# Two passes over the output weights: begun one set earlier, the second at three and four products a piece

## The chip, the cores and the metric

The kernel runs on one core of a Trainium2 chip. The metric is the device time of one execution in microseconds (us). A run of the kernel is told by the median of several executions; the profile is one more execution, recorded by the hardware profiler.

The engines are named as the profile names them: PE multiplies matrices (PEld is the loading of its stationary operand, which runs beside it), DVE is VectorE, ACT is ScalarE, POOL is GpSimd, SP is SyncE, which here only issues DMAs.

## The reference, cut to what matters

One decoder layer over x of 1024 tokens by 2048 features, in float32:

```python
h = einsum('bsd,dc->bsc', x, w_in) + b_in
q, k, v, g_attn, u_pool, g_pool = split(h)
a = banded_sink_attention(q, k, v, ...) * silu(g_attn)      # 16 heads, blocks of 128 queries
b = multiscale_pool(u_pool, w_pool, pool_scale) * silu(g_pool)
mix = einsum('bsc,cd->bsd', concatenate([a, b]), w_out)      # the output weights: w_out
ple = sigmoid(einsum('bsd,de->bse', x, w_gate_ple)) * einsum('bsp,pd->bsd', p_i, w_ple)
return layer_norm(2**0.25 * x + mix + ple, ln_gain, ln_bias)
```

The layer norm subtracts the mean over the 2048 features. So the mean over the output features may be taken out of each row of `w_out` beforehand. The kernel does that for the 1024 rows of the attention half (`a`): it writes a centred copy `wc` of these weights, which it reads instead of `w_out` in its last two stages.

## The kernel before, in words

**Jobs and products.** The large matrix products (with `w_in`, `w_gate_ple`, `w_out`) are cut into jobs. A job makes two blocks of 128 output features for 2 x 512 tokens, from half of the input features, in seven products instead of eight (Strassen's scheme in Winograd's form). So its operands are sums and differences of blocks: on the weights' side `s1` and the differences written over `raw` (`make_unit`), on the side of x the tiles `b11, b21, t1, t2, t3, b22, t4` (`set_from`). A float32 operand is split into a high and a low part (`wh` and `wl`, `b11h` and `b11l`, ...): ACT writes the high part, DVE the low one. A product is then 12 matmuls of 128x128 by 128x512: four slices of the contraction, three matmuls each, on lines 179 (high by high), 180 (wh by the low part of x) and 181 (wl by the high part of x). A unit is the pair `wh`, `wl` of one product; four units are made ahead of PE.

**Groups and sets.** Jobs run in groups of one to three. Jobs that run together alternate product by product. Group 0 holds three jobs (21 products), groups 1 and 2 two jobs each (14 products each); after those most groups are one job. The first two groups work on the first half of the contraction (the first set). During group 1 the second set is fetched, and during groups 1 and 2 its seven operands are made on ACT and DVE (the steps `s0` to `s4` of `set_from`). From group 3 on, attention (`heads`, 16 times, nine products apart) runs between the products of the large matrices. Its k and v are built twice (`k_build`, `v_build`), for the first and for the second group of heads.

**Banks.** A product accumulates in a bank of PSUM, `qa` or `qb`, each there twice. After it, ACT copies it into a tile `part` (L346) or DVE adds it (L122, `part<-part,qb`). A further product can begin in a bank only when that has been read. Transposes go to one bank `tr` that is there once: `trans` of attention uses it (ACT copies the high part, L544, then DVE makes the low part, `s<-tr,s`), and `v_build` (L457) too.

**Order.** A clock counts products: `tick` runs after each one what is due then. `after(n, fn)` puts `fn` at n products from now; `later` does the same and keeps its instructions behind the newest marked ones of each engine. So the place of each side task is a number in the code. The framework then orders each engine's instructions and adds the waits. Every engine works its list strictly in order, SP too: a DMA whose buffer isn't free holds up every DMA behind it.

**The two passes of `centre_weights`.** The weights come in 32 pieces of 128x512 (16 output blocks b, two halves h). There is one buffer for a piece, `cw`. First pass: for each piece a load (`fetch`, on SP) and two products later a row sum on DVE (`add_up`, L723), into `wsum`. Then the mean (`take_mean`). Second pass: the same load, two products later the subtraction on DVE in place (`centre`, L733, shown as L122 `cw<-cw,wmean`) and the store into `wc` on SP. Since `cw` is there once, the load of a piece waits for the row sum of the one before, and in the second pass for the end of the store before. In the kernel before, the passes are queued at clock 49, behind group 2 (`self.centre_weights(8, 3)`): first load due at 57, a piece every 2 products to 121; second pass from 123, at 2 products a piece where b is a multiple of 3 and at 3 otherwise, last subtraction due at 207.

Of the kernel before, what the change touches and what calls it, by code (L numbers as in the profile page):

```python
# [63 lines left out]
class Layer:  # L64
# [98 lines left out]
    def later(self, n, fn):  # L163

        def run():
            with ExitStack() as ctx:
                for ins in self.latest.values():
                    ctx.enter_context(self.tc.issue_after(ins))
                fn()
        self.after(n, run)  # L170
# [536 lines left out]

    def centre_weights(self, at, by):  # L710

        nc = self.nc
        cells = [(b, h) for b in range(NB) for h in range(2)]
        sums = self.fix.tile([P, 8, NB], F32, name="wsum")
        mean = self.fix.tile([P, 8], F32, name="wmean")
        now = []

        def fetch(b, h):
            now.append(self.load(self.tile(self.cw, [P, H], "cw"), self.wout[b, 0][:, h * H : h * H + H]))

        def add_up(b, h):
            k = now.pop().rearrange("p (k m) -> p k m", k=4)
            nc.vector.reduce_sum(sums[:, 4 * h : 4 * h + 4, b : b + 1], k, axis=mybir.AxisListType.X)  # L723

        def take_mean():
            nc.vector.reduce_sum(mean.rearrange("p (k b) -> p k b", b=1), sums, axis=mybir.AxisListType.X)
            nc.vector.tensor_scalar(out=mean, in0=mean, scalar1=1.0 / D, scalar2=None, op0=ALU.mult)

        def centre(b, h):
            w = now.pop()  # L730
            k = w.rearrange("p (k m) -> p k m", k=4)
            m = mean[:, 4 * h : 4 * h + 4].rearrange("p (k m) -> p k m", m=1).broadcast_to([P, 4, P])
            self.tt(k, k, m, ALU.subtract)  # L733
            self.load(self.wc[b, 0][:, h * H : h * H + H], w)

        for step in (add_up, centre):
            for c in cells:
                self.after(at, lambda c=c: fetch(*c))
                self.later(at + 2, lambda c=c, step=step: step(*c))
                at += by if step is centre and c[0] % 3 else 2  # L740
            if step is add_up:
                self.later(at + 1, take_mean)
                at += 2
# [96 lines left out]
    def run(self):  # L840
# [147 lines left out]
        nc.gpsimd.tensor_scalar(out=self.b8, in0=self.c(C_BIN, 8), scalar1=0.125, scalar2=1.0, op0=ALU.mult, op1=ALU.mult)  # L988
        begin, *steps = self.set_from(xs[1], T)
        begin()  # L990
        self.run_group(1)


# [8 lines left out]
        def build_kv(b, build, group):  # L1002
            src = [self.slot()[:, :T] for h in range(2)]
            for h in range(2):
                self.aside(src[h], kvd[b][:, h * T : h * T + T])
            self.later(2, lambda: build(group, src))
# [5 lines left out]
            self.after(t - 2 + 9 * i, lambda i=i: self.heads(i % 2, i // 2))  # L1012
        self.after(t + 63 + 8, lambda: build_kv(KB, self.k_build, 1))
        self.after(t + 63 + 22, lambda: build_kv(VB, self.v_build, 1))
        self.centre_weights(8, 3)
        begin, *steps = self.set_kept(xs[0], kept)
        for i in range(1, n2):
            if i == n2 - 1:
# [212 lines left out]
```

## Time and profile before

| what | value |
|---|---|
| time, median of 3 executions (lowest, highest) | 1488.71 us (1487.96, 1489.05) |
| the profiled execution's own time | 1488.72 us |
| its span | 1486.9 us |
| busy: PE, DVE, ACT, POOL | 1447.6, 1118.7, 779.5, 278.1 us |
| mean granted clock of PE | 0.992 |
| row sums on DVE (L723) | 32, from 174.3 to 376.4 us, median 680 ns |
| subtractions on DVE (`cw<-cw,wmean`) | 32, from 391.8 to 667.2 us, median 686 ns |

A busy PE isn't a PE at its best: a matmul of 128x512 is shown as about 390 ns long but they follow each other every 227 ns, so the busy times overlap. What the profile shows as a loss on PE is idle time, and a granted clock under 1.00. The profiled execution's time is 1.8 us over its span.

### The profile page before, as it was taken

Reading aid. Unit: us, or ns where it says so; the run is one execution under the profiler, and the core shown is the slowest. Engines: PE = TensorE matmul, PEld = TensorE weight load, DVE = VectorE, ACT = ScalarE, POOL = GpSimd, SP = SyncE. Lnnn points to the kernel's source line nnn. Section 1 sums busy time; section 2 is a strip of 40 time slices with the busy share of each in tenths; the row PEclk is TensorE's granted clock in tenths of the full one; section 3 lists DMA queues with packets and bytes.
Section 4 is the critical chain, followed back from the end, with each engine's and each line's share of the span. In section 5 each row is a group of like instructions: output and inputs, shape, how many; then the busy total and the mean of one; then the engine's idle time right before and its main releaser. Section 6 shows DMA issues by size and latency. Waiting matters only on the chain. (4 is left out here: it accounts for less than half of the span.)

```text
span 1486.9 us, 20458 instructions
## 1 busy us (share of the span) xinstructions
PE 1447.6 (97%) x6972; PEld 1223.5 (82%) x6972; DVE 1118.7 (75%) x2019; ACT 779.5 (52%) x1548; POOL 278.1 (19%) x388
## 2 busy tenths in 40 slices
PE   8999999999999999999999999999999999999996
PEld 6788888888887888888887778888877788899986
DVE  7788578888797878888667956565669666987786
ACT  5454666655666555666534443333256333554485
POOL 0000123332332333231111110000011111111231
PEclk9999999999999999999999999999999999999998
DMA  7563875445545455457856676666696768585464
GB/s 264 198 226 94 254 207 183 149 158 179 174 170 178 163 183 186 175 190 250 200 139 201 156 233 182 180 178 184 183 294 174 190 175 235 136 256 121 151 233 163
DMA packets 101913, 280.38 MB, mean 189 GB/s; under 512 B 11504, under 2 KB 17008, under 8 KB 101808
## 3 DMA queue, kind: packets, MB, share of 16 engines
q1 hardware_dynamic: 79024, 204.87, 40.3%
q0 software_dynamic: 19456, 66.86, 19.4%
q10 hardware_dynamic: 3328, 7.34, 1.5%
q8 instruction: 55, 0.90, 0.2%
q14 instruction: 50, 0.41, 0.1%
HBM read 193.04 MB, written 85.98 MB: 188 GB/s over the span
## 5 line engine op out<-in xcount | busy, mean ns | idle before, releaser
L222 ACT CAST wh<-raw 128x512 fp32r<-128x512 f32 x428 | 264.2, 619 | 448.6 <-PE qa L180 143.6
L122 DVE TENSOR_TENSOR wl<-raw,wh 128x512 fp32r<-128x512 f32 x428 | 299.5, 704 | 132.3 <-ACT wh L222 127.6
L346 ACT COPY part<-qa 128x512 f32<-128x512 f32 (+1 forms) x180 | 103.7, 576 | 56.5 <-PE qa L181 52.1
L551 POOL TENSOR_SCALAR_AFFINE_SELECT s<-s 128x512 fp32r<-128x512 f32 x128 | 100.6, 797 | 141.0 <-ACT s L544 98.3
L122 DVE TENSOR_TENSOR part<-part,qb 128x512 f32<-128x512 f32 (+1 forms) x120 | 80.9, 674 | 49.7 <-PE qb L181 47.0
L179 PE MATMUL qa<-b11h,wh 128*128 128x512 f32 (+2 forms) x292 | 111.2, 381 | 2.0 <-ACT b11h L248 1.5
L180 PE MATMUL qa<-b11l,wh 128*128 128x512 f32 (+2 forms) x292 | 110.2, 377 | 0.2 <-DVE b11l L122 0.2
L181 PE MATMUL qa<-b11h,wl 128*128 128x512 f32 (+2 forms) x292 | 109.8, 376 | 0.0
L179 PE MATMUL qb<-b21h,wh 128*128 128x512 f32 (+2 forms) x292 | 109.6, 375 | 0.0
L181 PE MATMUL qb<-b21h,wl 128*128 128x512 f32 (+2 forms) x292 | 109.2, 374 | 0.0
L180 PE MATMUL qb<-b21l,wh 128*128 128x512 f32 (+2 forms) x292 | 109.1, 374 | 0.0
L181 PE MATMUL qa<-t2h,wl 128*128 128x512 f32 (+1 forms) x260 | 100.0, 386 | 7.6 <-DVE wl L122 7.6
L179 PE MATMUL qa<-t2h,wh 128*128 128x512 f32 (+1 forms) x260 | 100.7, 388 | 5.3 <-ACT part L346 2.7
L179 PE MATMUL qb<-t1h,wh 128*128 128x512 f32 (+1 forms) x260 | 101.6, 391 | 3.5 <-DVE part L122 1.9
L181 PE MATMUL qb<-t1h,wl 128*128 128x512 f32 (+1 forms) x260 | 100.4, 386 | 1.5 <-DVE wl L122 1.5
L179 PE MATMUL qa<-t4h,wh 128*128 128x512 f32 (+1 forms) x260 | 100.3, 386 | 0.3 <-DVE part L122 0.3
L179 PE MATMUL qa<-t3h,wh 128*128 128x512 f32 (+1 forms) x260 | 100.5, 387 | 0.0
L180 PE MATMUL qb<-t1l,wh 128*128 128x512 f32 (+1 forms) x260 | 100.4, 386 | 0.0
L179 PE MATMUL qb<-b22h,wh 128*128 128x512 f32 (+1 forms) x260 | 100.3, 386 | 0.0
L180 PE MATMUL qb<-b22l,wh 128*128 128x512 f32 (+1 forms) x260 | 99.7, 384 | 0.0
L180 PE MATMUL qa<-t3l,wh 128*128 128x512 f32 (+1 forms) x260 | 99.7, 384 | 0.0
L181 PE MATMUL qb<-b22h,wl 128*128 128x512 f32 (+1 forms) x260 | 99.7, 383 | 0.0
(287 smaller groups left out, 3553.9 us busy)
## 6 DMA issues: line engine op xcount, KB each, us to landing
raw<-in_win SPq DMA_DIRECT2D x65, 512.0 KB, 4.0
h<-part SPq DMA_DIRECT2D x34, 512.0 KB, 2.9
part<-h POOLq DMA_DIRECT2D x34, 512.0 KB, 6.2
cw<-in_wout SPq DMA_DIRECT2D x64, 256.0 KB, 2.9
raw<-in_wgate SPq DMA_DIRECT2D x32, 512.0 KB, 4.4
raw<-wc SPq DMA_DIRECT2D x32, 512.0 KB, 4.1
s<-in_x SPq DMA_DIRECT2D x44, 256.0 KB, 5.7
wc<-cw SPq DMA_DIRECT2D x32, 256.0 KB, 2.3
```

Source lines behind the costliest of these rows:

```text
L122: return (eng or self.nc.vector).tensor_tensor(out=out, in0=a, in1=b, op=op)
L179: mm(ps, wh, xh, start=start, stop=False, skip_group_check=True)
L180: mm(ps, wh, xl, start=False, stop=False, skip_group_check=True)
L181: return mm(ps, wl, xh, start=False, stop=stop, skip_group_check=True)
L222: self.unit_latest = [nc.scalar.copy(out=hi, in_=src).ins, L.lo(lo, src, hi).ins]
L346: self.mark("ACT", self.nc.scalar.copy(out=dst, in_=ps))
L551: nc.gpsimd.affine_select(out=o4, in_=a4, pattern=[[0, 4], [sign, P]], compare_op=ALU.is_ge, fill=0.0, base=0 if side else -1, channel_mul ...
```

## The change

Three things change. `centre_weights` is queued behind group 0 (clock 21) instead of behind group 2 (clock 49), and its first load is due 2 products later instead of 8: at 23 instead of 57. The first pass keeps 2 products a piece and ends at 87. The second pass begins at 89, at 3, 4, 4, 4 products a piece in turn; its last subtraction stays due at 207. The instructions are the same in number and kind.

```diff
-    def centre_weights(self, at, by):
+    def centre_weights(self, at):
...
         for step in (add_up, centre):
-            for c in cells:
+            for i, c in enumerate(cells):
                 self.after(at, lambda c=c: fetch(*c))
                 self.later(at + 2, lambda c=c, step=step: step(*c))
-                at += by if step is centre and c[0] % 3 else 2
+                at += 2 if step is add_up else 3 + (i % 4 > 0)
             if step is add_up:
                 self.later(at + 1, take_mean)
                 at += 2
...
         begin()
+        self.centre_weights(2)
         self.run_group(1)
...
-        self.centre_weights(8, 3)
         begin, *steps = self.set_kept(xs[0], kept)
```

The lists of PE and POOL are the same before and after, instruction by instruction. Those of DVE, ACT and SP differ. In the rows below a name's number tells buffers apart and has no other meaning.

**DVE in group 2**, where the second set's operands are made: the low part of t2 (`t2l`), the units (`wl`), the sums and differences of the weights (`s1`, `raw`), and the reading of the bank of the job's second product (`part<-part,qb`). Before:

```order
L122 TENSOR_TENSOR wl_289_1095<-raw_269_998,wh_288_1094 128x512
L122 TENSOR_TENSOR s1_291_1112<-raw_264_962 128x512
L122 TENSOR_TENSOR t2l_305_1185<-two_236_813,t2h_304_1184 128x1024
L122 TENSOR_TENSOR raw_264_962<-raw_221_720,raw_264_962 128x512
L122 TENSOR_TENSOR wl_293_1118<-s1_291_1112,wh_292_1117 128x512
L122 TENSOR_TENSOR raw_221_720<-s1_291_1112,raw_221_720 128x512
L122 TENSOR_TENSOR s1_297_1143<-raw_270_1000 128x512
L122 TENSOR_TENSOR raw_221_720<-raw_221_720 128x512
L122 TENSOR_TENSOR raw_270_1000<-raw_269_998,raw_270_1000 128x512
L122 TENSOR_TENSOR wl_299_1149<-s1_297_1143,wh_298_1148 128x512
L122 TENSOR_TENSOR raw_269_998<-s1_297_1143,raw_269_998 128x512
L122 TENSOR_TENSOR part_280_1076<-part_280_1076,qb_300_1152 128x512
```

The same stretch of DVE's list now:

```order
L122 TENSOR_TENSOR wl_296_1117<-raw_273_1011,wh_295_1116 128x512
L122 TENSOR_TENSOR s1_298_1134<-raw_267_972 128x512
L122 TENSOR_TENSOR t2l_314_1213<-two_236_815,t2h_313_1212 128x1024
L122 TENSOR_TENSOR raw_267_972<-raw_221_720,raw_267_972 128x512
L122 TENSOR_TENSOR wl_300_1140<-s1_298_1134,wh_299_1139 128x512
L122 TENSOR_TENSOR raw_221_720<-s1_298_1134,raw_221_720 128x512
L723 TENSOR_REDUCE wsum_790<-cw_286_1096 128x4
L122 TENSOR_TENSOR raw_221_720<-raw_221_720 128x512
L122 TENSOR_TENSOR s1_305_1168<-raw_274_1013 128x512
L122 TENSOR_TENSOR part_287_1098<-part_287_1098,qb_308_1177 128x512
```

A row sum (L723) stands in it, and the reading of the bank has moved ahead of the difference over `raw` of the second job, of the unit behind it and of one more difference.

**SP in groups 1 and 2**: the loads of the weights (`raw<-in_win`), the stores of the first set's partial products (`h<-part`) and the loads of pieces (`cw<-in_wout`). Before:

```order
L136 DMA h_6_99<-part_154_323 128x1024
L136 DMA raw_264_962<-in_win 128x1024
L136 DMA raw_269_998<-in_win 128x1024
L136 DMA raw_270_1000<-in_win 128x1024
L136 DMA raw_273_1019<-in_win 128x1024
L136 DMA h_7_100<-part_228_790 128x1024
L136 DMA h_9_102<-part_230_792 128x1024
L136 DMA h_8_101<-part_229_791 128x1024
L136 DMA h_10_103<-part_231_793 128x1024
L136 DMA raw_318_1270<-in_win 128x1024
```

And now:

```order
L136 DMA h_6_99<-part_154_323 128x1024
L136 DMA cw_251_889<-in_wout 128x512
L136 DMA cw_260_932<-in_wout 128x512
L136 DMA raw_267_972<-in_win 128x1024
L136 DMA cw_268_975<-in_wout 128x512
L136 DMA raw_273_1011<-in_win 128x1024
L136 DMA raw_274_1013<-in_win 128x1024
L136 DMA cw_275_1016<-in_wout 128x512
L136 DMA raw_278_1035<-in_win 128x1024
L136 DMA h_7_100<-part_228_792 128x1024
L136 DMA h_9_102<-part_230_794 128x1024
L136 DMA cw_281_1055<-in_wout 128x512
```

Each load of a piece now stands between these loads and stores; it waits for the row sum of the piece before it, and holds up what stands behind it.

**DVE where k and v are built for the second group of heads**. The rows around the subtraction of a piece (`cw<-cw,wmean`) some products ahead of it, before:

```order
L514 TENSOR_SCALAR st_897_4373<-st_897_4373 128x4
L122 TENSOR_TENSOR st_897_4373<-cst_75,st_897_4373 128x4
L122 TENSOR_TENSOR part_923_4508<-part_923_4508,qa_926_4513 128x512
L122 TENSOR_TENSOR cw_938_4599<-cw_938_4599,wmean_1411 128x512
L122 TENSOR_TENSOR wl_955_4684<-raw_849_4120,wh_954_4683 128x512
L122 TENSOR_TENSOR s1_962_4718<-raw_891_4349 128x512
```

And now:

```order
L514 TENSOR_SCALAR st_905_4405<-st_905_4405 128x4
L122 TENSOR_TENSOR st_905_4405<-cst_75,st_905_4405 128x4
L122 TENSOR_TENSOR part_930_4538<-part_930_4538,qa_933_4543 128x512
L122 TENSOR_TENSOR wl_962_4710<-raw_857_4152,wh_961_4709 128x512
L122 TENSOR_TENSOR s1_968_4742<-raw_899_4379 128x512
L122 TENSOR_TENSOR st_905_4405<-st_905_4405 128x2
```

The subtraction between the reading of the bank and the unit is gone from here. Some rows further, at the low part of the transposed probabilities (`s<-tr,s`), whose end frees `tr` for `v_build`, DVE's list before:

```order
L122 TENSOR_TENSOR raw_849_4120<-raw_849_4120 128x512
L122 TENSOR_TENSOR wl_964_4724<-raw_849_4120,wh_963_4723 128x512
L525 RECIPROCAL st_897_4373<-st_897_4373 128x2
L122 TENSOR_TENSOR cw_959_4705<-cw_959_4705,wmean_1411 128x512
L122 TENSOR_TENSOR s_967_4748<-tr_965_4742,s_966_4747 128x512
L122 TENSOR_TENSOR wl_975_4778<-s1_962_4718,wh_974_4777 128x512
L122 TENSOR_TENSOR v0_971_4772<-tr_970_4767,v0_971_4772 128x4x64
```

And now:

```order
L122 TENSOR_TENSOR raw_857_4152<-raw_857_4152 128x512
L122 TENSOR_TENSOR wl_970_4748<-raw_857_4152,wh_969_4747 128x512
L122 TENSOR_TENSOR cw_960_4705<-cw_960_4705,wmean_791 128x512
L122 TENSOR_TENSOR st_905_4405<-st_905_4405 128x2
L122 TENSOR_TENSOR wl_981_4804<-s1_968_4742,wh_980_4803 128x512
L122 TENSOR_TENSOR s_973_4774<-tr_971_4768,s_972_4773 128x512
L525 RECIPROCAL st_905_4405<-st_905_4405 128x2
L122 TENSOR_TENSOR v0_977_4798<-tr_976_4793,v0_977_4798 128x4x64
```

Here a subtraction still stands ahead of `s<-tr,s`, and so does now the unit that stood behind it.

## The prediction

> **What bounds the kernel now.** I read the page first, then busy times by stage, then what PE waited for in the stages that the change reaches, then the tile `cw` and the neighbourhood of the one long wait.
>
> ```profile
> span 1486.9 us, 20458 instructions
> PE 1447.6 (97%) x6972; PEld 1223.5 (82%) x6972; DVE 1118.7 (75%) x2019; ACT 779.5 (52%) x1548; POOL 278.1 (19%) x388
> ```
>
> PE is the bound: its list is the same before and after, so only its idle time, 1486.9 - 1447.6 = 39.3 us, and lost clock can change. The stages: group 0; groups 1 and 2, into which the first pass now moves; the first pass as it was; the second pass; the rest.
>
> ```profile
> core 0: us, PE busy (x) PEld busy (x) DVE busy (x) ACT busy (x) POOL busy (x), PEclk, DMA share, GB/s
> 0.00:73.00 73.00, 65.17 (x267) 51.50 (x268) 53.41 (x69) 35.49 (x52) 1.64 (x9) 0.98 0.63 234
> 73.00:149.00 76.00, 76.00 (x337) 62.91 (x336) 62.94 (x82) 38.45 (x59) 1.96 (x2) 1.00 0.49 159
> 149.00:391.00 242.00, 241.95 (x1197) 203.69 (x1196) 187.79 (x442) 147.43 (x356) 66.50 (x86) 1.00 0.58 180
> 391.00:671.00 280.00, 276.34 (x1385) 233.32 (x1384) 227.91 (x534) 174.37 (x443) 89.60 (x112) 0.99 0.53 184
> 671.00:1487.00 816.00, 788.18 (x3792) 672.06 (x3790) 586.68 (x894) 383.72 (x641) 118.43 (x179) 0.99 0.67 191
> ```
>
> The second column is PE's busy time. From 73 to 391 us PE has nothing to give: the first pass costs nothing where it stands now. In the second pass PE idles 280 - 276.34 = 3.66 us and its clock is under 1. What it waited for from 73 to 690 us (sum, count, longest):
>
> ```profile
> PE tr L457 <- DVE s L122: 2.4, 1, 2.4
> PE qb L179 <- DVE part L122: 0.8, 1, 0.8
> PE qa L181 <- DVE wl L122: 0.7, 1, 0.7
> PE qa L179 <- ACT part L346: 0.5, 1, 0.5
> ```
>
> So 4.4 us in four places, and one is more than half of it. That is all the wait the change can reach, beside the clock.
>
> **The change part by part.** The passes on DVE and SP:
>
> ```profile
> L136 SPq DMA_DIRECT2D cw<-in_wout x64: 327/332/1613, 31.2 to 662.5; - x64
> L723 DVE TENSOR_REDUCE wsum<-cw x32: 672/680/689, 174.3 to 376.4; 128x4 f32<-128x512 f32 x32
> L122 DVE TENSOR_TENSOR cw<-cw,wmean x32: 677/686/1123, 391.8 to 667.2; 128x512 f32<-128x512 f32 x32
>   DMA cw<-in_wout: 14.7, 12
> DMA to landing us min/median/max: 2.0/2.7/6.7
> ```
>
> Beside its 64 instructions the passes made DVE stand idle 14.7 us in 12 places, since a subtraction or sum at the head of DVE's list waits there for its load.
>
> (1) *Second pass thinned.* It now spans products 89 to 207 (118) instead of 123 to 207 (84). Counted in DVE's list from the place where the 128th unit is made on, 22 subtractions stand where 32 stood: 10 x 0.69 = 6.9 us of DVE less in the stage from 391 us. At the long wait it looks so:
>
> ```profile
> 456.40 0.69 DVE L122 TENSOR_TENSOR part<-part,qa 128x512 f32<-128x512 f32 x1
> 456.57 0.60 ACT L222 CAST wh<-raw 128x512 fp32r<-128x512 f32 x1
> 458.87 0.77 DVE L122 TENSOR_TENSOR cw<-cw,wmean 128x512 f32<-128x512 f32 x1 [1.78 <-DMA cw<-in_wout]
> 459.56 1.23 DVE L122 TENSOR_TENSOR wl<-raw,wh 128x512 fp32r<-128x512 f32 x1
> 464.88 0.69 DVE L122 TENSOR_TENSOR wl<-raw,wh 128x512 fp32r<-128x512 f32 x1
> 465.66 0.69 DVE L122 TENSOR_TENSOR cw<-cw,wmean 128x512 f32<-128x512 f32 x1
> 466.27 0.68 DVE L122 TENSOR_TENSOR s<-tr,s 128x512 fp32r<-128x512 f32 x1
> 464.20 0.40 PE L180 MATMUL qa<-b11l,wh 128*128 128x512 f32 x1
> 467.01 1.11 PE L457 MATMUL tr<-ident,s 128*128 128x128 f32 x4 [2.42 <-DVE s L122]
> ```
>
> PE stands at `v_build`'s transposes from 464.60 to 467.01 because DVE frees `tr` at 466.95. DVE works there without a pause since 458.87, and began late: 1.78 us of waiting for a piece and 0.77 us for the piece. In the new list this subtraction is gone, and the unit behind it, whose `wh` is ready at 456.57 + 0.60 = 457.17, starts at 457.2 instead of 459.56: 2.4 us earlier. The later subtraction (465.66) stays ahead of `s<-tr,s`, and so does now one more unit, a step of 466.27 - 465.66 = 0.6 us. So `tr` is free at 466.95 - 2.4 + 0.6 = 465.2 and PE waits 465.2 - 464.6 = 0.6 us: 1.8 us gained. The ends: 0 us gained if ACT or the scores hold DVE's list up behind the unit, 2.4 us if all the wait goes. I take 1.8, which is worked out along the list.
>
> (2) *The clock.* PE's idle time in windows of 3.4 us, and the clock granted in the window and in the next:
>
> ```profile
> 40.10:43.50 3.40, 2.15 (x9) 1.78 (x10) 3.40 (x5) 1.58 (x2) 0.00 (x0) 1.00 0.78 308
> 43.50:46.90 3.40, 3.40 (x16) 2.80 (x16) 3.40 (x4) 1.98 (x4) 0.00 (x0) 1.00 0.05 18
> 463.40:466.80 3.40, 1.20 (x6) 0.63 (x4) 3.36 (x10) 2.21 (x4) 0.00 (x0) 1.00 0.79 293
> 466.80:470.20 3.40, 3.19 (x11) 2.80 (x12) 1.28 (x4) 1.13 (x3) 1.27 (x2) 0.51 0.53 193
> 879.90:883.30 3.40, 1.92 (x8) 1.61 (x9) 2.49 (x4) 1.95 (x4) 0.00 (x0) 1.00 0.97 378
> 883.30:886.70 3.40, 3.40 (x16) 2.82 (x15) 0.69 (x1) 2.41 (x4) 0.00 (x0) 1.00 0.60 173
> 1108.60:1112.00 3.40, 1.36 (x5) 0.92 (x6) 3.40 (x6) 1.15 (x3) 1.12 (x2) 0.99 1.05 386
> 1112.00:1115.40 3.40, 3.40 (x10) 2.66 (x9) 3.40 (x4) 0.00 (x0) 0.00 (x0) 0.50 1.05 408
> ```
>
> Idle 3.40 - 1.20 = 2.20 and 3.40 - 1.36 = 2.04 us were followed by a window at half clock; 3.40 - 1.92 = 1.48 and 1.25 us were not. So the long wait also cost 3.4 x (1 - 0.51) = 1.7 us of PE, and a wait of 0.6 us would not. Ends: 0 and 1.7; I take 1.7, as 0.6 us is far below 1.48.
>
> [...]
>
> (3) *The other three waits*, 0.8 + 0.7 + 0.5 = 2.0 us. At each the list of DVE keeps a subtraction at the same place among the units (ahead of the one of 0.7 us a subtraction behind the same unit and the same reading of a bank) or stands behind the last piece with the same rows. I take 0; ends 0 and 2.0 gained.
>
> (4) *First pass moved into groups 1 and 2.* Twelve sums now stand between the units made from 85 to 145 us: 12 x 0.68 = 8.2 us, against 76 - 62.94 = 13.1 us in which DVE idles there. But it doesn't idle evenly:
>
> ```profile
> 110.00:120.00 10.00, 10.00 (x46) 8.29 (x45) 10.00 (x15) 6.13 (x10) 0.00 (x0) 1.00 0.27 107
> 119.96 0.68 DVE L122 TENSOR_TENSOR part<-part,qb 128x512 f32<-128x512 f32 x1
> 121.76 0.39 PE L179 MATMUL qb<-t1h,wh 128*128 128x512 f32 x1
> 122.90 0.68 DVE L122 TENSOR_TENSOR part<-part,qb 128x512 f32<-128x512 f32 x1
> 124.48 0.39 PE L179 MATMUL qb<-t1h,wh 128*128 128x512 f32 x1
> ```
>
> DVE is full (third busy column) while it makes the second set. The two readings of `qb` end 121.76 - 120.64 = 1.1 and 124.48 - 123.58 = 0.9 us before PE needs the bank again. Three sums land ahead of the first, 2.0 us, which would eat that cover. But the list has also moved the first reading ahead of three operations (a difference, a unit, a difference: 3 x 0.6 = 1.8 us), and the second likewise ahead of half of `t3l`. So the readings stay within 0.2 us of their times, and the lateness falls on `t3l`, `b22l` and `t4l`, which wait a product or more for PE. Cost 0; if that cover goes, every us of lateness beyond 0.9 us is one on PE. SP: a dozen loads of pieces now stand among the loads of `raw` and stores of `h`. SP waits there anyway; each load is held by one sum (0.68 us), and the weights are four units ahead. On POOL nothing moves, and ACT carries no piece. Cost 0 (ends 0 and the price in the rival below).
>
> (5) *From 149 to 391 us* the same rhythm of sums, then 10 subtractions where 17 sums stood: 0, since PE idles 0.05 us there. The stores grow into this stretch, in a DMA share of 0.58. The last piece stays due at product 207, and its reader begins at 1245 us:
>
> ```profile
> L136 SPq DMA_DIRECT2D raw<-wc x32: 319/320/1568, 1245.4 to 1456.4; - x32
> ```
>
> Sum: -1.8 - 1.7 = -3.5 us. Against the profiled execution's own 1488.72 us (span 1486.9 and 1.8 around it; the median of the runs is 1488.71, the same): 1485.2 us.
>
> **The rivals.**
>
> *The clock falls all the same* (17 in 100). [...] Price 1.7: 1488.7 - 1.8 = 1486.9 us.
>
> *The gain is hidden or taken back* (17). For it: a unit now stands ahead of `s<-tr,s`, ACT's list has moved there too, and 2.04 us of idle would already halve the clock. A new wait of 1 to 3 us between 150 and 670 us would look the same; against it, DVE has less to do from 300 us on. 1488.4 us.
>
> *More goes* (7): the 0.6 us left over in (1) and the 2.0 us of (3): 1485.2 - 2.6 = 1482.6 us.
>
> *Slower: the sums starve DVE while the second set is made* (11). A piece's cycle is sum, issue, landing: 0.68 + 0.33 + L. It is due every two products, 2 x (124.48 - 121.76) = 5.44 us, so from L = 4.4 us on each piece holds DVE's whole list up, units and banks with it. With eight pieces between 104 and 142 us and 0.9 us of cover the loss is 8 (L - 4.4) - 0.9; it outweighs 3.5 us, with 3.0 us more for a visible loss, from L = 5.3 us on. For it: the longest landing was 6.7 us, and pieces now queue behind `raw` and `h` on SP. Against: the median is 2.7, and the DMA share is 0.27 from 110 to 120 us. At L = 5.3: 1488.7 - 3.5 + 6.3 = 1491.5 us.
>
> **How the numbers follow.** My forecast has 48 in 100 and its own range is 1483.9 to 1486.2, from the ends of (1). 0.2% of 1488.7 is 3.0 us, about what the measurement can tell from no change: faster means under 1485.7. Of the forecast's 48 some 36 lie there, with the 7 of "more goes" and 2 of the others: faster 0.45. Slower than 1491.7 takes most of the last rival and a new wait with a half window: 0.09. The rest, 0.46, is within. The range, 1482.7 to 1490.0, leaves out the far ends of "more goes" and of the slower case.
>
> **What would show it.** Right: no idle of PE over 1 us between 73 and 680 us, no half clock before 1112 us, `tr` L457 waiting under 1 us; DVE busy about 71 us from 73 to 149 us with PE at 76; DVE's waits for `cw` loads well under 14.7 us. [...]

## Result: slower by 0.66%

| | before | after |
|---|---|---|
| time, median of 6 executions (lowest, highest) | 1489.01 us (1487.96, 1493.04) | 1500.42 us (1495.51, 1500.85) |
| ratio, 95% interval | | 1.0066 [1.0053, 1.0078] |
| profiled execution: time, span | 1488.72, 1486.9 us | 1500.85, 1499.1 us |
| mean granted clock of PE | 0.992 | 0.986 |

The changed kernel is slower, outside the range that was given: by 9.8 us from the ratio (7.9 to 11.6), and the medians are 11.4 us apart. The page of the profile after, span and busy times:

```profile
span 1499.1 us, 20461 instructions
PE 1455.3 (97%) x6972; PEld 1228.3 (82%) x6972; DVE 1120.7 (75%) x2019; ACT 780.1 (52%) x1548; POOL 275.8 (18%) x388
```

The work is the same; DVE has only 2.0 us more of it. The stages of the changed kernel (columns: time, busy PE, PEld, DVE, ACT, POOL, then granted clock, DMA share, GB/s):

```profile
73.00:149.00 76.00, 76.00 (x337) 62.95 (x336) 68.24 (x93) 38.23 (x58) 1.96 (x2) 1.00 0.60 194
149.00:199.00 50.00, 43.05 (x179) 33.91 (x178) 26.08 (x46) 23.24 (x38) 6.93 (x10) 0.93 0.86 230
199.00:400.00 201.00, 201.00 (x1008) 170.05 (x1007) 160.27 (x387) 124.62 (x318) 58.82 (x76) 1.00 0.53 172
400.00:690.00 290.00, 288.27 (x1455) 243.68 (x1454) 234.29 (x547) 180.60 (x454) 91.81 (x116) 1.00 0.50 172
```

One stage of 50 us has lost 50 - 43.05 = 6.95 us of PE and some of its clock; from 73 to 149 us and from 199 to 400 us PE has no gap. What PE waited for from 73 to 690 us (sum, count, longest):

```profile
PE qa L181 <- DVE wl L122: 3.5, 2, 2.8
PE qa L179 <- DVE part L122: 2.8, 1, 2.8
PE tr L457 <- DVE s L122: 1.0, 1, 1.0
PE qb L179 <- ACT part L346: 1.0, 1, 1.0
```

Two waits of 2.8 us are new, and both are for DVE; a wait of 1.0 us for ACT and one of 0.4 us make up the rest of the 6.95. DVE's list and PE's at these two places:

```profile
169.50 0.69 DVE L723 TENSOR_REDUCE wsum<-cw 128x4 f32<-128x512 f32 x1 [4.47 <-DMA cw<-in_wout]
170.70 0.68 DVE L122 TENSOR_TENSOR part<-part,qa 128x512 f32<-128x512 f32 x1
171.43 0.62 PE L179 MATMUL qa<-t4h,wh 128*128 128x512 f32 x1 [2.75 <-DVE part L122]
185.45 0.69 DVE L723 TENSOR_REDUCE wsum<-cw 128x4 f32<-128x512 f32 x1 [5.87 <-DMA cw<-in_wout]
190.05 1.88 DVE L122 TENSOR_TENSOR wl<-raw,wh 128x512 fp32r<-128x512 f32 x3
190.79 0.50 PE L181 MATMUL qa<-t3h,wl 128*128 128x512 f32 x1 [2.78 <-DVE wl L122]
```

DVE stands for 4.47 and for 5.87 us at a row sum whose load hasn't landed. The reading of bank `qa` and the units `wl` stand behind that sum in DVE's list, and PE waits for them. The tile `cw` from 143 to 196 us:

```profile
  DMA cw<-in_wout: 22.6, 5
DMA to landing us min/median/max: 2.6/6.8/8.2
```

Five waits at row sums, 22.6 us of DVE, and a median landing of 6.8 us where the prediction counted with 2.7. Not each of them reaches PE: behind the first, 4.60 us at 154.21 us, PE has no idle time. The windows behind the two long waits of PE:

```profile
168.30:171.70 3.40, 0.65 (x3) 0.27 (x2) 2.21 (x4) 0.00 (x0) 0.00 (x0) 0.99 1.00 336
171.70:175.10 3.40, 3.40 (x9) 2.63 (x9) 2.86 (x5) 0.62 (x1) 0.06 (x1) 0.50 1.02 414
188.70:192.10 3.40, 1.31 (x6) 1.10 (x7) 3.34 (x7) 1.30 (x3) 0.00 (x0) 1.00 0.23 72
192.10:195.50 3.40, 2.96 (x10) 2.04 (x9) 2.33 (x5) 0.41 (x2) 0.00 (x0) 0.51 0.92 225
```

Each wait was followed by a window at half clock, 2 x 1.7 = 3.4 us. So this stage lost 6.95 + 3.4 = 10.4 us.

At `v_build` the forecast gain is there (the wait, and the window after it):

```profile
478.05 0.55 PE L457 MATMUL tr<-ident,s 128*128 128x128 f32 x3 [1.04 <-DVE s L122]
480.30:483.70 3.40, 3.40 (x21) 2.91 (x20) 2.21 (x10) 3.35 (x14) 1.91 (x3) 1.00 0.13 49
```

1.04 us where 2.42 us stood, and no half clock: 1.4 + 1.7 = 3.1 us gained. Together 10.4 - 3.1 = 7.3 us of the 12.2 between the two spans.

Where the rest lies can be read too, since PE's list is the same before and after: each matmul of the changed kernel can be set beside its twin, the same one in the kernel before. What starts at 48 us in the kernel before starts 1.95 us later in the changed one, and so does what starts at 160 us; at 200 us it is 12.62 us later, at 400 us 12.71, at 480 us 9.75, at 760 us 9.0, at 890 us 11.1 and at the end 12.2. So by this measure the stage cost 10.7 us and the way from 400 to 480 us gave 3.0. The other 4.5 us lie outside these two places: 1.95 us before the first row sum (87 us), some 2 us near 890 us and some 1 us behind that, less 0.7 from 480 to 690 us. The clock has four more half windows there than before (one each near 10, 42, 892 and 1124 us). The first 1.95 us aren't the change's doing as far as is seen: in e1 below, which has the same first pass, it is 0.05 us at the same place.

Why the loads landed late is seen in the DMA issues from 145 to 190 us (count, KB each, median us to landing). Before:

```profile
part<-h POOLq DMA_DIRECT2D x6, 512.0 KB, 7.7
cw<-in_wout SPq DMA_DIRECT2D x3, 256.0 KB, 4.2
```

And after:

```profile
part<-h POOLq DMA_DIRECT2D x6, 512.0 KB, 8.3
cw<-in_wout SPq DMA_DIRECT2D x6, 256.0 KB, 7.0
q<-part SPq DMA_DIRECT2D x2, 512.0 KB, 10.0
```

In this stretch POOL adds the first set's partial products, which come back from memory (`part<-h`, a DMA that adds to what stands in its target), and the groups' other results go out. In the kernel before, the DMA engines were as good as full here already:

```profile
150.00:160.00 10.00, 10.00 (x46) 8.29 (x45) 3.01 (x5) 4.73 (x8) 2.87 (x4) 1.00 0.93 230
160.00:170.00 10.00, 10.00 (x46) 8.29 (x45) 6.46 (x10) 4.57 (x9) 2.99 (x5) 1.00 0.97 320
170.00:180.00 10.00, 10.00 (x47) 8.02 (x47) 6.01 (x9) 9.29 (x15) 0.47 (x1) 1.00 0.95 221
```

### The profile page after: what moved, and what is told of

Read it like the earlier page. It is cut to its first block, busy times and chain, and to the rows that moved or that the text cites. A ratio compares the mean times of both kernels' runs of the same rounds, so it can differ in the third digit from the quotient of the medians.

```text
span 1499.1 us, 20461 instructions
## 1 busy us (share of the span) xinstructions
PE 1455.3 (97%) x6972; PEld 1228.3 (82%) x6972; DVE 1120.7 (75%) x2019; ACT 780.1 (52%) x1548; POOL 275.8 (18%) x388
## 5 line engine op out<-in xcount | busy, mean ns | idle before, releaser
L181 PE MATMUL qa<-t3h,wl 128*128 128x512 f32 (+1 forms) x260 | 100.2, 385 | 2.8 <-DVE wl L122 2.8
L180 PE MATMUL qa<-t2l,wh 128*128 128x512 f32 (+1 forms) x260 | 100.8, 389 | 0.0
L180 PE MATMUL qa<-t4l,wh 128*128 128x512 f32 (+1 forms) x260 | 100.4, 386 | 0.0
```

The source lines that it names most:

```text
L180: mm(ps, wh, xl, start=False, stop=False, skip_group_check=True)
L181: return mm(ps, wl, xh, start=False, stop=stop, skip_group_check=True)
```

## The experiments

The theory, called A: DVE works in order, so a row sum whose load is late holds up the readings and units behind it; the loads are late at 146 to 190 us because the adding DMAs (A1) fill the DMA engines there. Its rivals: the sums' own time on DVE is too much for this stretch; the thinned second pass is to blame; or the pieces' traffic delays other transfers, whoever reads the pieces. All edits are against the changed kernel; ratios are to the kernel before, run beside it on the same chip (medians there 1491.99, 1490.27 and 1490.85 us in the three sets of runs).

**The early start alone**, with the old spacing of the second pass (e1):

```diff
-                at += 2 if step is add_up else 3 + (i % 4 > 0)
+                at += 3 if step is centre and c[0] % 3 else 2
```

> The first pass begun in the first set, the second pass at the spacing of before (2 or 3 products a piece, so that it ends at product 173). Theory A (the loss lies between 146 and 200 us: DVE stands at a row sum whose load lands after 5.6 to 8.2 us, because POOL's adding DMAs and SP's loads fill the DMA queues there): the loss of the changed kernel between 145 and 200 us stays, 7 us of PE idle and one or two half clocks, so slower than before by 8 to 13 us. Theory B (the thinned second pass causes part of the loss): faster than the changed kernel by several us.

Measured 1501.93 us, ratio 1.0067 [1.0046, 1.0088], as theory A had it. PE idles 1.64 us twice and then once for long, in the same stretch:

```profile
191.73 0.79 PE L181 MATMUL qa<-t3h,wl 128*128 128x512 f32 x1 [6.76 <-DVE wl L122]
190.20:197.00 6.80, 5.27 (x14) 4.21 (x15) 5.27 (x10) 0.55 (x2) 0.00 (x0) 0.50 0.63 158
```

The whole loss is here without the thinned pass, and `v_build` waits 2.75 us with a half window as in the kernel before. The thinned second pass isn't to blame.

**The thinned second pass alone**, begun at the old place (e2):

```diff
-        self.centre_weights(2)
...
+        self.centre_weights(8)
         begin, *steps = self.set_kept(xs[0], kept)
```

> The first pass where it was (behind group 2), the second pass at 3, 4, 4, 4 products a piece, so that it ends at product 243. Theory A: no idle of PE between 145 and 200 us; the wait at v_build near 467 us shrinks to under 1 us and the half clock behind it goes: 1485 us, 3 to 4 us faster than before, less what the pieces cost that now stand in the next set's beginning near 680 us (0 to 1.5 us). Theory B: slower than before.

Measured 1491.86 us, ratio 1.0001 [0.9988, 1.0014]: not 3 to 4 us faster, less 0 to 1.5, as A had it, and not slower, as B had it. No loss between 73 and 423 us; `v_build` waits 0.78 us and keeps its clock. But the second pass now ends at 766 us instead of 667, in the next stage, and there the same thing happens to a subtraction (DVE's row, PE's row, the window behind):

```profile
750.85 0.69 DVE L122 TENSOR_TENSOR cw<-cw,wmean 128x512 f32<-128x512 f32 x1 [3.39 <-DMA cw<-in_wout]
752.26 0.79 PE L179 MATMUL sc<-e,s 128*128 128x512 f32 x1 [4.19 <-DVE s L653]
752.20:755.60 3.40, 3.34 (x8) 2.66 (x9) 2.24 (x5) 0.00 (x0) 1.15 (x2) 0.50 0.88 280
```

A load that is 3.39 us late for DVE costs PE 4.19 us and half a window. So the thinning gives 1.6 us and a half window at `v_build`, and the later end of the pass takes more back at one late load.

**A pause in the first pass** (e4): after its 12th piece, 12 products without a piece; everything behind it ends 12 products later.

```diff
+                if step is add_up and i == 11:
+                    at += 12
```

> The changed kernel with a pause of 12 products in the first pass, after its twelfth piece: no sum between products 47 and 61 (about 147 to 180 us); both passes end 12 products later. Theory A: the DVE waits of 2.5 to 5.9 us for loads of pieces go, PE idles under 1 us between 73 and 400 us, and the gain at 467 us stays: 1484 to 1487 us. Rival C (the twelve sums in groups 1 and 2 are already too many for DVE while it makes the second set): a loss stays, over 1490 us.

Measured 1488.68 us, ratio 0.9980 [0.9965, 0.9996]. No sum waits from 143 to 196 us, and PE's largest idle there is 1.06 us, just over the 1 us expected; `v_build` waits 0.61 us. The sums are all still made; that they and their loads stay out of the crowded stretch takes most of the loss away. Not all of it: set beside their twins in the kernel before, PE's matmuls still fall back 2.0 us from 160 to 200 us (10.7 in the changed kernel).

**The loads of five pieces left out**, pieces 13 to 17, the sums kept on older data (e5; their five sums aren't those of the reference):

```diff
-            now.append(self.load(...))
+            if len(seen) not in range(12, 17):
+                last[:] = [self.load(...)]
...
+            now.append(last[0])
```

> The changed kernel without the loads of pieces 13 to 17 (those that landed late); their row sums read the twelfth piece again, so DVE has all its sums at the same places. Left out: five loads, and with them the right mean. Theory A: the sums wait for nothing, PE idles under 1 us between 73 and 400 us: 1484 to 1487 us. Rival C (the sums' own 0.68 us each is too much for DVE): the loss stays, about 1498 us.

Measured 1489.53 us, ratio 0.9985 [0.9970, 1.0000]. All that PE waited for from 73 to 690 us:

```profile
PE qb L179 <- DVE part L122: 0.8, 1, 0.8
PE tr L457 <- DVE s L122: 0.8, 1, 0.8
PE qa L181 <- DVE wl L122: 0.7, 1, 0.7
PE tr L457 <- DVE v L122: 0.6, 1, 0.6
```

The sums stand at the same places in DVE's list as in the changed kernel, and the loss is gone. Their own time isn't the cause; their loads are. One part of the expectation missed: DVE still stands 3.78 us at 177.88 us, at the next piece that is loaded (its load lands after 8.9 us). PE's only idle time near it is 0.6 us, so a late load costs PE only where something that PE needs soon stands behind it.

**The sums of the same pieces left out**, their loads kept (e6; the mean lacks five pieces):

```diff
+        nc.gpsimd.memset(sums, 0.0)
...
+            done.append(b)
+            if len(done) - 1 in range(12, 17):
+                return
```

> The changed kernel without the row sums of pieces 13 to 17, their loads kept (left out: these five sums; the mean is wrong). The same bytes go through the queues, DVE has nothing at its head that waits for them. Theory A: PE idles under 1.5 us between 73 and 400 us, though the loads land late. Rival D (the traffic of the pieces itself holds up the loads of weights and the adding DMAs): PE still idles 5 us or more there.

Measured 1497.47 us, ratio 1.0049 [1.0028, 1.0071]: a miss for A, which had the loss gone. DVE no longer waits at these pieces, but PE idles 5.20 us at 189.88 us. ACT's row and DVE's ahead of it:

```profile
181.21 0.69 DVE L727 TENSOR_REDUCE wsum<-cw 128x4 f32<-128x512 f32 x1 [4.66 <-DMA cw<-in_wout]
187.32 0.62 ACT L485 CAST s<-s 64x512 fp32r<-64x512 f32 x1 [4.02 <-DMA s<-q]
187.97 1.40 DVE L122 TENSOR_TENSOR s<-s,s 64x512 fp32r<-64x512 f32 x2 [4.27 <-ACT s L485]
189.88 0.48 PE L457 MATMUL tr<-ident,s 128*128 128x128 f32 x1 [5.20 <-DVE v L122]
```

Without a sum between them only their own landing spaces the loads: five go out one behind the other from 145 to 169 us, landing after 3.3 to 8.5 us. The next sum that is made finds its load late again. ACT waits 4.02 us for its q (`s<-q`), the low part of which DVE makes ahead of the `v` that PE waits for. This transfer isn't slow itself, it lands after 3.0 us; it goes out late. The stores of q stand behind the pieces' loads in SP's list and are issued at 174.58 us instead of 165.48 in the changed kernel, and the reading back, which waits for them, at 184.34 instead of 175.00. So the third rival is half right: the pieces' loads also reach PE by way of SP's list, which they hold up, whoever reads the pieces. This edit moved two things at once (no sums, and other DMAs later in SP's list), and doesn't part them; how much of the changed kernel's own loss comes by this second way, no run shows.

**The adding DMAs left out** (e8), ten `part<-h`; the second set's results then lack the first set's:

```diff
-        self.nc.gpsimd.dma_start(out=t, in_=job.first(job.b[i]), accum_op=ALU.add)
+        if not (job.w is self.win and job.half == 1):
+            self.nc.gpsimd.dma_start(out=t, in_=job.first(job.b[i]), accum_op=ALU.add)
```

> The changed kernel without the ten DMAs of POOL that add the first set's partial products to the q, k and v jobs of the second set (left out: that sum, so q, k and v hold the second half of the contraction alone). Loads of pieces and sums stay where they are. Theory A1 (those adding DMAs, 8.3 us each, are what makes the loads of pieces land after 5.6 to 8.2 us from 146 to 190 us): the loads land after about 3 us, DVE waits under 1 us for each, PE idles under 1 us between 73 and 400 us. Rival A2 (SP's own loads of weights and stores of q ahead of the pieces do it): landings of 5 to 8 us stay, and PE idles 5 us or more.

Measured 1486.75 us, ratio 0.9975 [0.9963, 0.9987], some of it for the work left out. The issues of pieces from 145 to 190 us, and the tile `cw` from 143 to 196 us:

```profile
cw<-in_wout SPq DMA_DIRECT2D x8, 256.0 KB, 2.8
  DMA cw<-in_wout: 2.8, 3
```

Eight loads of the same size at the same place land after 2.8 us instead of 7.0, and DVE's wait falls from 22.6 to 2.8 us (2.03 the longest, where under 1 was expected). From 73 to 420 us PE has no idle time left. A1 holds: the adding DMAs make the loads late. Whether it is their adding or merely their bytes isn't shown, since both went.

**More lead** (e9): for the loads due 24 to 37 products after the passes are queued, a piece every four products, with four products between load and sum.

```diff
-                self.later(at + 2, ...)
-                at += 2 if step is add_up else 3 + (i % 4 > 0)
+                lead = 4 if 24 <= at < 38 else 2
+                self.later(at + lead, ...)
+                at += lead if step is add_up else 3 + (i % 4 > 0)
```

> The changed kernel with a piece every four products, and its sum four products behind its load, between products 45 and 61; both passes end 8 products later. The loads stay in the crowded stretch (three of them), but have 10.9 us to land instead of 5.4. Theory A: with landings of 5.6 to 8.2 us DVE waits under 1 us; PE idles under 2 us between 73 and 400 us; 1484 to 1488 us on the scale of the first runs, 0.1 to 0.3% faster than before. If the pieces' presence there costs by itself: slower than before by 0.2% or more.

Measured 1489.93 us, ratio 0.9994 [0.9981, 1.0007]: the 0.1 to 0.3% that A had it faster aren't shown, nor is the loss of the other side. The landings from 143 to 196 us, and what PE waited for behind ACT:

```profile
DMA to landing us min/median/max: 2.5/6.3/8.6
PE qa L179 <- ACT part L346: 1.0, 1, 1.0
PE qb L179 <- ACT part L346: 0.6, 1, 0.6
```

The loads land as late as in the changed kernel (8.05, 6.30, 8.58 us), but no sum waits for one in this stretch, and PE idles 1.6 us there instead of 6.95, with no half clock (2.2 us lost by the twins, instead of 10.7). So late loads in themselves cost little as long as they are few and spaced, and DVE isn't made to stand at them. Which of these does most isn't parted: the edit has fewer loads in the stretch, further apart and with more lead.

**A longer pause and three products throughout** (e7): five pieces, a pause to 38 products after the passes are queued, the other sums at 2 a piece, then the second pass at 3.

```diff
-                at += 2 if step is add_up else 3 + (i % 4 > 0)
+                at += 2 if step is add_up else 3
+                if step is add_up and i == 4:
+                    at = 38
```

> A version that may beat both: five sums between products 25 and 34 (ahead of the stretch in which DVE makes the second set), none until product 61, the other 27 from there at 2 products a piece, the second pass at 3 products a piece, ending at product 212. Theory A: no DVE wait over 1 us for a piece between 73 and 200 us, v_build waits under 1 us and no half clock follows it: 0.15 to 0.3% faster than before. If the gain at v_build needs the wider spacing of 3, 4, 4, 4: the 2.4 us wait and the half clock stay, and the time is that of before.

Measured 1489.69 us, ratio 0.9998 [0.9987, 1.0009]. No idle of PE over 0.5 us from 73 to 400 us; `v_build` waits 1.34 us without a half window. By these rows it should have been faster, and A had it 0.15 to 0.3% faster: a miss. Its profiled execution had six half windows in four places outside them (near 41, 881, 1110 and 1424 us).

**The pause of e4 once more** (e10):

> The kernel of the pause of 12 products once more, in more rounds, to see whether it lies under the kernel before. By theory A (row sums that wait for late loads cost the 11 us, and the thinned second pass gives 1 to 3 us at `v_build`) its time is 0 to 3 us under the kernel before, a ratio of 0.998 to 1.0, and no row of PE's idle time between 73 and 420 us is over 1.1 us. By the rival that the ratio of 0.998 was scatter of the half-clock windows between executions, the ratio comes to 0.9995 to 1.0005.

Measured 1487.58 us, ratio 0.9981 [0.9963, 0.9998]: the same as the first time, on another chip. The waits from 73 to 690 us:

```profile
PE qb L179 <- DVE part L122: 1.5, 2, 1.1
PE qb L179 <- ACT part L346: 1.2, 1, 1.2
PE tr L457 <- DVE s L122: 0.6, 1, 0.6
PE qa L179 <- ACT part L346: 0.3, 1, 0.3
```

Of the versions that leave nothing out, it is the only one that lies under the kernel before, by 3.3 us both times. The rival's ratios, 0.9995 to 1.0005, lie above the measured one, though the interval reaches into them. The row of 1.2 us is just over the 1.1 expected.

**The pause, and the second pass at three products throughout** (e11):

```diff
-                at += 2 if step is add_up else 3 + (i % 4 > 0)
+                at += 2 if step is add_up else 3
+                if step is add_up and i == 11:
+                    at += 12
```

> The pause of 12 products, and the second pass at three products a piece throughout, so that it ends some 24 products sooner. Theory A expects that the sums stay free of the crowded stretch, as with the pause alone, so no idle of PE over 1.1 us from 73 to 420 us. At `v_build` the wait should be 0.6 to 1.4 us (1.34 with three a piece and a longer pause). Time within 2 us of the pause alone, ratio 0.997 to 1.0. The rival: the denser subtractions, which run behind the pause at products 75 to 180, make DVE late at the waits of PE behind `part` and `wl` from 250 to 420 us, then an idle row of over 1.5 us stands there and the ratio is over 1.001.

Measured 1491.18 us, ratio 1.0012 [0.9993, 1.0031]. Neither side was right: PE idles 1.51 and 1.54 us at 167 and 180 us, more than A expected, and nothing over 0.6 us from 250 to 420 us, where the rival put its wait. `v_build` waits 0.74 us. The wait near 1115 us, after the pass, was 3.56 us in this profile and 2.18 in that of e10; it follows the landing of another load (`s<-pre`). From 160 to 200 us PE fell back 3.4 us behind its twins, where e10 lost 1.8. Why this version isn't faster stays open.

**All runs by the same measure.** Set beside its twins in the kernel before, PE falls back from 160 to 200 us by 10.7 us in the changed kernel and 13.5 in e1; by 9.5 in e6; by 2.0 in e4, 1.8 in e10, 2.2 in e9 and 3.4 in e11; by 0.7 in e5; and by less than 0.1 in e2, e7 and e8. So it is 9.5 us and more where pieces are loaded at two products or closer beside the adding DMAs from 145 to 175 us, and 3.4 us at most in all others.

## Why the prediction was wrong

**Steps (1) and (2), right.** The late subtraction ahead of `v_build` was the cause of its wait: 2.42 became 1.04 us (0.6 forecast), and without it no half window follows. In e2, e5, e8, e9 and e10 it is 0.6 to 0.8 us, and in e1, which keeps the old spacing, 2.75 with a half window. The half window went with the wait, as the rows of step (2) had it. The rival in which the clock falls all the same came true beside them, at another place: the wait at 881 us, in the kernel before 2.21 us and split over two windows (1.48 us in the longer part), was 2.62 us in the changed kernel, at 890.89. There 2.39 us of it lay in one window, from 888.5 us, and the next was granted 0.50.

**Step (3), right in kind.** The waits of 0.7 and 0.8 us stay, as 0.68 and 0.84; the one of 0.5 us is gone.

**Step (4), right in its own stretch.** "Cost 0" was worked out for the twelve sums from 85 to 145 us. There it held: PE 76.00 of 76 us, DVE's waits for pieces 1.4 us from 73 to 149 us, and at 160 us PE is as far behind its twins as at 48 us.

**Step (5), wrong: the step that failed.** It put the sums from 149 to 391 us at 0, because "the same rhythm of sums" ran there and PE idled 0.05 us. It didn't run in all of it: in the kernel before the first row sum starts at 174.3 us, and the moved pass has sums at 154, 163 and 169.5 us. And it left out, as step (4) did, that a load may land after its sum is due; only the slower rival priced that, and for another stretch. The DMA share of 0.58 is a mean over 242 us, and hid 30 us with a share of 0.93 to 0.97. Of the first pass's own loads, three fell between 145 and 190 us in the kernel before, landing after 4.2 us; the median of 2.7 was taken from 64 loads spread over 630 us. Five loads now landed there after 5.6 to 8.2 us, DVE stood 22.6 us at their sums, and the cost was 10.4 us (10.7 by the twins), not 0.

**The slower rival had the mechanism, and the wrong place.** It gave the loss as n (L - 4.4) - 0.9. With the landings of 7.20, 8.19, 5.62, 6.85 and 7.62 us of the five pieces it comes to 13.5 - 0.9 = 12.6 us. That this is near the 10.4 measured is partly luck: the rule counts waits alone, and these came to 6.95 us; the other 3.4 are clock. The rival had 11 in 100 since the landing was judged by the median of all loads and by the share from 110 to 120 us.

**What was to show it.** DVE at 71 us from 73 to 149 us: 68.2. DVE's waits for loads of pieces well under 14.7 us: 28.7, twice as long. No idle over 1 us up to 680 us: three. No half clock before 1112 us: six windows, where the kernel before has two; two of the six are behind the sums. PE waiting for `part` and `wl` behind landings over 4.4 us, by which the slower rival loses, came at 171 and 191 us, some 30 us and more behind the pieces from 104 to 142 us that it priced.

**The forecast as it would be with its step mended.** With the sums out of the crowded stretch (e4, e10) the gain is 3.3 us twice, against the 3.5 forecast. This agrees with steps (1) and (2), but that the figures are so near is partly luck. In the profile of e10 the twins show 4.3 us gained from 300 to 480 us, 3.1 of them from 460 to 480 us, around `v_build`, and 2.9 us lost from 100 to 200 us; the rest of its gain lies behind 1100 us, where the kernel before has a half window. And e7 has the gain at `v_build` too, and a ratio of 0.9998.

**What stays open.** The two places make 7.3 us, the ratio 9.8 (7.9 to 11.6). In e1 the same sum, 10.0 us idle and 3.4 of clock, is above its 10.0 (6.9 to 13.1). Half windows elsewhere differ between executions of one kernel: the profiled runs of e4 and e10 (same code) have six and one on record outside the end, 1491.43 and 1487.03 us. (The record of e10's clock begins at 13.2 us; its matmuls before that are 0.43 us apart, as in the half window of the changed kernel from 42.0 us, where at full clock they are 0.23 apart, so the two counts can't be compared at the start.) The one behind the wait at 881 us is in six of the eleven profiles of the changed kernel and its variants and not in that of the kernel before. Whether the four extra windows of the changed kernel come in most of its executions, one profile can't tell.

## What to carry to other kernels

A side task that is moved earlier passes through every stage in between: read the DMA share and the landing times in windows of 10 us along its whole new path, not its medians over the old one. An engine that works in order must not have, at the head of its list, the reading of a load that may be late (here DVE stood 22.6 us at five of them, and PE 2.75 and 2.78 us behind two): give the load more lead in a full stretch, or leave that stretch out. The same holds for the engine that issues the DMAs: a load that waits for its buffer holds up those behind it (in e6 the stores of q went out at 174.58 us instead of 165.48). A long wait on an engine that sets the end costs more than its length where half a clock window follows it (here 1.7 us more behind 2.75 and 2.78 us).

## What the runs showed of the hardware

An idle PE of 2.7 us was followed by half clock in one execution and not in the next. It is the same wait, near 42 us in the same code, e4 first and then e10. The windows of e10 are an estimate, counted back from its half window at 880.2 us in steps of (1434.60 - 41.96) / 408 = 3.413 us. That step is worked out from the changed kernel, whose clock fell to half at 41.96, 171.66, 192.14, 891.88 and 1434.60 us, 38, 6, 205 and 159 steps apart.

```profile
39.50:42.90 3.40, 0.72 (x4) 0.49 (x4) 3.40 (x5) 2.29 (x3) 0.00 (x0) 1.00 0.47 186
42.90:46.30 3.40, 3.40 (x10) 2.66 (x8) 3.40 (x4) 0.18 (x1) 0.00 (x0) 0.50 0.31 123
37.10:40.50 3.40, 1.67 (x8) 1.05 (x6) 3.40 (x4) 1.90 (x3) 0.00 (x0) 1.00 0.01 2
40.50:43.90 3.40, 2.44 (x11) 2.02 (x12) 3.40 (x6) 1.36 (x3) 0.00 (x0) 1.00 0.78 308
43.90:47.30 3.40, 3.40 (x17) 2.81 (x16) 3.40 (x4) 2.24 (x5) 0.00 (x0) 1.00 0.14 55
```

In e4 the 2.68 us lie in one window and the next is at 0.50; in e10 a boundary splits 2.69 us into 1.73 and 0.96, and the clock stays. Where the boundaries fall differs between executions (39.5 and 42.9 us in e4; 37.1, 40.5 and 43.9 in e10). No sharp limit comes out of the traces. Windows with 1.61 us of idle time (e4, from 1111.3 us) and 1.72 us (e5, from 29.1 us) were followed by half clock, windows with 1.83 (e9, from 876.0 us) and 1.89 us (e2, from 1107.2 us) were not; in the kernel before and the changed one each one with 2.0 us or more was, from where their record of the clock begins (the least of them 2.04 us, from 1108.6 us before, and 2.09, from 188.7 us after). And at 1422.6 us in the kernel before the clock halved behind a window in which the profile shows no idle time of PE (3.40 us busy of 3.40), but, from 1419.7 us on, matmuls of 128x1.

With adding DMAs of 512 KB beside them, loads of 256 KB landed after a median of 7.0 us in the changed kernel, and after 2.8 us where ten of these were left out (e8).
